# A chunked recurrence: score products alternate between row halves of TensorE, the old state is scaled on GpSimd, low-rank factors share the array, dense steps stand between chain steps

## The chip, the cores and the metric

One Trainium2 chip, one of its cores. The metric is the device time of one execution in microseconds (us); lower is better. TensorE (PE in the rows; PEld is its weight load) does the matrix products, VectorE (DVE), ScalarE (ACT) and GpSimd (POOL) the rest, SyncE (SP) issues nearly all transfers.

## What is computed

Two transformer layers and a third block on 512 tokens of width 1024, all in float32. The part that the change touches is the time mixing of the first layer:

```python
r, k, v = xr @ w_rkv[0], xk @ w_rkv[1], xv @ w_rkv[2]
w = -softplus(-(w0 + tanh(xw @ w1) @ w2)) - 0.5        # w1: 1024 x 64
a = sigmoid(a0 + (xa @ a1) @ a2)                       # a1: 1024 x 64
...
def step(S, inp):                                      # 16 heads, S is 64 x 64 per head
    sa = einsum('bhij,bhj->bhi', S, -kk_t)
    S = S * w_t + sa * b_t + v_t * k_t
    return S, einsum('bhij,bhj->bhi', S, r_t)
```

followed by a group norm, a gate and an output projection. Before and after it stand gated feed-forward networks, and behind it window attention and the third block, which the change does not touch.

## The kernel before

The recurrence runs over chunks of 64 tokens. A unit is 128 tokens (two chunks, c = 0 and 1) and 8 of the 16 heads; there are 8 units, n = 0 to 7, two for each 128 tokens, and m = 2 (n // 2) + c numbers the chunks from 0 to 7. For a unit four stages are written as generators that yield between steps:

- stage a: cumulative decays (`psc`), then the scores (`sc`, L1072). A pair of heads lies on 128 partitions, one on the lower 64 rows and one on the upper; f = 0 to 3 numbers the pairs. For each chunk the products of the four lower heads go to one bank of PSUM, a yield follows, then the four upper ones go to another. DVE multiplies each bank by a mask (L1074). The pool `pa` has two banks. Then come transposes (`pt`).
- stage b: inverts the triangular blocks, first on DVE, one 16-block per lane, then by small products in 32 x 32 tiles (`psG`, `psW`).
- stage c: per chunk a chain: products with the old state and the scores (`xy`, L1181 and L1184), L1189, L1194, then the new state in `st`: for each row half a product of the identity with the old state (L1203) and four products (L1206) are summed in PSUM, and DVE multiplies by the decay (L1209). The chunk behind it reads the new state.
- stage d: group norm and gate; the unit's output goes to DRAM (L1247).

`Rwkv.run` calls them in rounds. `chain(n)` strings the four stages together; stage x of unit n starts behind stage x of unit n - 1; at most three units (later two) hold a slot. In a round every live chain makes one step, then three dense steps follow (four in the second part). The dense side of the first part is `dense(1, ...)`: projections and low-rank paths of the second 256 tokens, beside units 0 to 3. The dense side of the second part is `first_half(...)`: output projection, norm and feed-forward network of the first 256 tokens, beside units 4 to 7; it reads the outputs of units 0 to 3. `dense(0, ...)` has run before the recurrence, without a chain beside it. What comes behind the second part (the output projection of the second 256 tokens) reads the outputs of units 4 to 7.

In `dense`, `mixes` makes the mixed inputs xr, xw, xa, xk, xv, xg in this order, 8 tiles each, on DVE. `low_rank` sums 8 products with xw and 8 with xa in one bank; the weight block for xw is w1 beside 64 columns of zeros, the one for xa is 64 columns of zeros beside a1, so that the results lie on the lower and on the upper partitions. A float32 product is two instructions on PE in the rows (the 128 score products stand as x256).

The order in which each engine runs its instructions is made by the framework, from the order in which they are emitted and a simulated timeline (`schedule_with_timeline_sim=True`, L2021): an instruction can overtake those emitted before it on its engine.

Of the kernel before, what the change touches and what calls it, by code (L numbers as in the profile page):

```python
# [17 lines left out]
P = 128  # L18
T = 512
# [53 lines left out]


class Turns:
    """tiles of PSUM from these pools in turn"""
# [9 lines left out]
class Net:  # L86
    def __init__(self, tc, ctx, ins, outs):
# [21 lines left out]
        # 1 / rms of h by tokens, for products with h before its norm's division  # L109
# [36 lines left out]
    def weights(self, src, pool=None, cols=1024, hl=None):  # L146
        """src: DRAM AP [P, cols] -> (hi, lo) tiles [P, cols] of float32r"""
# [29 lines left out]
    def rstd(self, ps, dim, out=None):  # L177
        """1 / sqrt(sum / dim + eps) of the sums, on every partition; in ps itself or in out"""
# [37 lines left out]
    def sumsq(self, pieces, n):  # L216
        """sum over pieces of piece^2, [P, n]"""
# [28 lines left out]
    def rms(self, half, onpe=False):  # L246
        """self.rx of this half"""
# [12 lines left out]
    def pairs(self, pool, tag="xn", **k):  # L260
        """8 tiles [P, 2, 256] out of four slots"""
# [29 lines left out]
    def post(self, g, half):  # L291
        """emit g now for the first half, later for the second, beside the phase that follows"""
# [20 lines left out]
    def ffn(self, idx, gpost, after_half, side=(), early=()):  # L313
        nc = self.nc
        win, wout = self.ins["ffn_w_in"][idx], self.ins["ffn_w_out"][idx]
        with ExitStack() as es:
# [4 lines left out]
            for fh in range(2):  # L321
# [12 lines left out]
                # the first tiles by halves of the tokens, beside the tail of the phase before  # L334
# [40 lines left out]
                # out: 88 blocks (d, f) in 11 pieces of 8  # L375
# [35 lines left out]
class Halves:  # L411
    """an FFN by halves of the tokens: its steps as generators"""
# [4 lines left out]
    def hidden(self, f, halves, w=None):  # L417
        """hidden tile f for each (x, a, half): x 8 times [P, 2, 256], a the pair of hi and lo [P, 256]"""
# [17 lines left out]
    def out(self, fh, halves):  # L436
        """output tiles of half fh of the hidden ones; halves: (a by f, sink(d, psum))"""
# [15 lines left out]
def lay(inputs):  # L453
    """host-side layout only"""
# [11 lines left out]
    # query heads in the order in which tile t = 4 a + j holds heads (2 a, j) and (2 a + 1, j)  # L466
# [11 lines left out]
    # second block: columns of the input projection by tiles; the rotary key part four times over  # L478
# [21 lines left out]
    l1 = np.stack([np.concatenate([g("rwkv_w1")[0], z64], 1), np.concatenate([z64, g("rwkv_a1")[0]], 1), g("rwkv_g1")[0]])  # L500
    o["lora1"] = np.ascontiguousarray(l1.reshape(3, 8, 128, 128).transpose(0, 2, 1, 3)).reshape(3, 128, 1024)
# [11 lines left out]
class Rwkv:  # L513
    def __init__(self, N):
# [3 lines left out]
        # 64-blocks of ones on the diagonal, and the inclusive triangle within chunks of 64  # L518
# [4 lines left out]
        # tri[s, t] = 1 where t >= s within the same chunk  # L523
# [3 lines left out]
        # masks of the scores, rows s (both halves alike), columns [r | a] for even chunks and [a | r] for odd ones  # L527
# [16 lines left out]
    def unorm(self, gcol, half):  # L544
# [8 lines left out]
        if half == 0:  # L553
            # on demand of the projections
# [18 lines left out]
    def dense(self, hf, tmp, exact, mx, mxe):  # L573
        """r, k, v and the low-rank paths of one half of the tokens, to DRAM; emitted in steps.
        exact: projections with products of the float32 operands as they are, the others with those of their
        halves hi and lo. mx, mxe: how many mixed inputs of each kind fit, and how to make room for one"""
# [21 lines left out]
        def mixes():  # L598
            for i, out, ex in order:
                for k in range(KT):  # L600
# [20 lines left out]
        # the weights in the order of their use, loaded ahead of it  # L621
        srcs = [(N.ins["w_rkvo"][j, o], j in exact) for j in range(3) for o in range(KT)] + [(N.ins["lora1"][2], True), (N.ins["lora2"][1], True)]
# [13 lines left out]
        def proj(j, x, post):  # L636
            """post(o, psum) is a generator that runs beside the next products"""
            ex = j in exact
            o = 0
            while o < KT:  # L640
                # the first two together: their inputs come one by one
# [31 lines left out]
        def low_rank():  # L673
            psl = mmt()
            ws = [weights(N.ins["lora1"][j], True) for j in range(2)]
            yield from lora(ws[0], xw, psl[:, :n], True, False)
            yield from lora(ws[1], xa, psl[:, :n], False, True)
# [27 lines left out]
        def post_k(o, ps):  # L705
# [5 lines left out]
            # k (a k_a + 1 - k_a)  # L711
# [11 lines left out]
            # kk over its norm, and times a  # L723
# [43 lines left out]
        order = [(0, xr, 0 in exact), (1, xw, True), (4, xa, True), (2, xk, 1 in exact), (3, xv, 2 in exact), (5, xg, True)]  # L767
# [32 lines left out]
    def run(self, h_spill, gpost, gpre, ffn, gffn, after_half):  # L800
        """the block, and the FFN that follows it"""
# [44 lines left out]
        def step():  # L846
            live[:] = [g for g in live if next(g, live) is not live]
# [7 lines left out]
        more = True  # L855
        run(islice(side, 1))
        while more or ("d", 2) not in at:
# [3 lines left out]
            step()  # L861
            for _ in range(3):
                more = more and next(side, side) is not side
# [9 lines left out]
        more = True  # L873
        while n < 8 or live:
# [3 lines left out]
            step()  # L878
            if ("d", 3) in at:
                for _ in range(4):  # L880
                    more = more and next(side, side) is not side
        for _ in side if more else ():
            pass
# [60 lines left out]
    def out_half(self, hf, y, m, h_spill, gpost, after):  # L944
        """output projection, norm and residual of one half of the tokens"""
# [14 lines left out]
    def first_half(self, h_spill, gpost, gpre, ff, m, a, xA):  # L960
        """for the first half of the tokens: output projection, and the lower half of the hidden tiles"""
# [23 lines left out]
class Core:  # L985
    """recurrence over chunks of 64 tokens; unit n: tokens 128 (n // 2) on, heads 8 (n % 2) on"""

    def __init__(self, R, dram, cx):
# [16 lines left out]
        # 64-blocks of 16 (chunk, head) pairs, 4160 apart: their diagonal 16-blocks are then 1040 apart throughout  # L1005
        self.us, self.wsd = ([dram.tile([16, 4160], F32, name=f"{x}{n}") for n in range(2)] * 4 for x in ("us", "wsd"))
        zero = self.S0[0].rearrange("p a b -> p (a b)")[:, 0:520]
        for w in self.wsd[:2]:
            nc.gpsimd.dma_start(out=w.rearrange("a (b e) -> (a b) e", e=520), in_=zero)
# [12 lines left out]
    def load(self, nm, n, t, c=None):  # L1022
        """feature-major [P, 4, tokens of chunk c or of both]"""
# [4 lines left out]
    def stage_a(self, n, G):  # L1028
# [9 lines left out]
        # columns of chunk c: [r | a] and [k | b] for the even one, [a | r] and [b | k] for the odd one  # L1038
# [23 lines left out]
        # scores  # L1062
# [3 lines left out]
        for c in range(2):  # L1066
            s = st_.tile([P, 8, P], F32, tag=f"S{c}", name="S")
            for p in range(2):
                ps = pa("sc").rearrange("p (f t) -> p f t", t=P)
                rows = slice(64 * p, 64 * p + 64)  # L1070
                for f in range(4):
                    nc.tensor.matmul(ps[:, f, :], lhsT=two(kb, rows, f, c), rhs=two(ar, rows, f, c), start=f == 0, stop=True, skip_group_check=True)  # L1072
                yield
                nc.vector.tensor_tensor(out=s[:, p:8:2, :], in0=ps, in1=R.mask[c][:, None, :].to_broadcast([P, 4, P]), op=ALU.mult)  # L1074
# [950 lines left out]
```

## Time and profile before

| | us |
|---|---|
| median of 3 runs | 2792.01 |
| lowest and highest | 2785.80, 2796.27 |
| span of the profiled execution | 2792.8 |

The profiled execution's span is 0.8 us above the median of the three runs. In the trace the rows of a timeline join neighbouring instructions of one line: the time is from the start of the first to the end of the last. PE's products are pipelined and their ends are modelled, so that what one costs is read from start to start. PEclk is the granted clock as a share of 2.4 GHz.

### The profile page before, as it was taken

The page shows a single profiled execution, that of the slowest core. Times are in us where ns is not written, and L with a number is a line of the kernel's source. Part 1 is how long each engine was busy: PE and PEld are TensorE (multiplying, and loading weights), DVE is VectorE, ACT ScalarE, POOL GpSimd, SP SyncE. Part 2 cuts the span into 40 slices and gives each one's busy share as a digit, 9 for nine tenths or more (in the row PEclk, how much of TensorE's full clock was granted, in tenths as well). Part 3 has the DMA queues.
Part 4 walks back from the last instruction along what each step waited for, and adds up shares of the span by engine and source line. Part 5 has one row for each costly group of instructions (what it writes and reads, how often), then busy time and mean ns, then how long its engine had stood idle before and what let it go on. Part 6 is the DMA issues. An engine that isn't in the chain of part 4 may idle for free.

```text
span 2792.8 us, 43747 instructions
## 1 busy us (share of the span) xinstructions
PE 2709.0 (97%) x17518; PEld 2355.8 (84%) x17518; DVE 1472.3 (53%) x2964; ACT 1169.9 (42%) x2073; POOL 12.5 (0%) x30
## 2 busy tenths in 40 slices
PE   8999998899999999999999999999999999999998
PEld 7888887778888999999988889789888898777887
DVE  7724466455547546448652446547524465334555
ACT  5223326244346554335532234446322334454643
POOL 0000000000000000000000000000000000000000
PEclk9999999998999999999999999899999999999999
DMA  6622316854574453235442233002322232123333
GB/s 211 211 96 97 113 65 215 251 164 117 176 228 129 133 190 136 91 107 181 133 144 91 98 106 136 34 18 89 107 98 95 101 104 101 64 69 103 116 124 101
DMA packets 207716, 345.26 MB, mean 124 GB/s; under 512 B 66196, under 2 KB 136212, under 8 KB 207512
## 3 DMA queue, kind: packets, MB, share of 16 engines
q1 hardware_dynamic: 206920, 341.65, 37.6%
q8 instruction: 138, 2.26, 0.3%
q14 instruction: 66, 0.54, 0.1%
q0 software_dynamic: 160, 0.53, 0.0%
q10 hardware_dynamic: 432, 0.28, 0.0%
HBM read 299.56 MB, written 41.26 MB: 122 GB/s over the span
## 4 chain that ended last, share of the span: by engine, by line
PE 88%; DMA 4%; DVE 4%; ACT 3%; issue 1%; SPq 0%; DVEq 0%; ACTq 0%
PE gu L165 11%; PE gu L164 11%; PE gu L166 11%; PE o L164 8%; PE o L166 8%; PE o L165 8%; PE ps L594 4%; PE ps L166 2%; PE ps L164 2%; PE ps L165 2%; PE psg L164 1%; PE psg L165 1%; PE psg L166 1%; PE po L1417 1%; PE sc L1072 1%
## 5 line engine op out<-in xcount | busy, mean ns | idle before, releaser
L153 ACT ACTIVATE whl<-wr 128x1024 fp32r<-128x1024 f32 x417 | 439.0, 1059 | 729.9 <-PE gu L166 408.1
L154 DVE TENSOR_TENSOR whl<-wr,whl 128x1024 fp32r<-128x1024 f32 x417 | 507.9, 1222 | 373.3 <-ACT whl L153 370.9
L164 PE MATMUL gu<-xn,whl 128*128 128x512 f32 (+1 forms) x1200 | 436.5, 366 | 7.8 <-ACT xn L242 7.1
L165 PE MATMUL gu<-xn,whl 128*128 128x512 f32 (+1 forms) x1200 | 439.8, 367 | 3.6 <-DVE xn L243 3.6
L166 PE MATMUL gu<-xn,whl 128*128 128x512 f32 (+1 forms) x1200 | 438.6, 366 | 0.8 <-DVE whl L154 0.8
L166 PE MATMUL o<-a,whl 128*128 128x256 f32 (+1 forms) x906 | 297.9, 330 | 0.0
L165 PE MATMUL o<-a,whl 128*128 128x256 f32 (+1 forms) x906 | 297.2, 329 | 0.0
L164 PE MATMUL o<-a,whl 128*128 128x256 f32 (+1 forms) x906 | 296.4, 329 | 0.0
L164 PEld LDWEIGHTS gu<-xn,whl 128*128 128x128 f32 x1200 | 226.8, 190 | 43.8 <-ACT xn L242 7.3
L165 PEld LDWEIGHTS gu<-xn,whl 128*128 128x128 f32 x1200 | 228.3, 190 | 40.2 <-DVE xn L243 4.8
L166 PEld LDWEIGHTS gu<-xn,whl 128*128 128x128 f32 x1200 | 228.4, 190 | 37.1 <-DVE whl L154 1.2
L165 PE MATMUL gu<-pair,whl 128*128 128x256 f32 x704 | 200.1, 285 | 1.1 <-DVE pair L243 1.1
L166 PE MATMUL gu<-pair,whl 128*128 128x256 f32 x704 | 198.3, 282 | 1.2 <-DVE whl L154 1.2
L164 PE MATMUL gu<-pair,whl 128*128 128x256 f32 x704 | 199.4, 285 | 0.0
L165 PEld LDWEIGHTS o<-a,whl 128*128 128x128 f32 x906 | 170.8, 189 | 17.1
L166 PEld LDWEIGHTS o<-a,whl 128*128 128x128 f32 x906 | 170.8, 189 | 16.9
L164 PEld LDWEIGHTS o<-a,whl 128*128 128x128 f32 x906 | 170.4, 189 | 17.1
L594 PE MATMUL ps<-mxe,wraw 128*128 128x256 f32 x608 | 153.9, 405 | 11.5 <-DVE mxe L608 5.8
L594 PEld LDWEIGHTS ps<-mxe,wraw 128*128 128x128 f32 x608 | 119.4, 203 | 33.1 <-DVE mxe L608 6.0
L166 PEld LDWEIGHTS gu<-pair,whl 128*128 128x128 f32 x704 | 133.4, 189 | 2.1 <-DVE whl L154 1.4
L165 PEld LDWEIGHTS gu<-pair,whl 128*128 128x128 f32 x704 | 133.1, 189 | 2.3 <-DVE pair L243 1.7
L164 PEld LDWEIGHTS gu<-pair,whl 128*128 128x128 f32 x704 | 132.6, 189 | 1.5 <-issue 0.4
(438 smaller groups left out, 4783.5 us busy)
## 6 DMA issues: line engine op xcount, KB each, us to landing
wr<-in_ffn_w_in_dram SPq DMA_DIRECT2D x204, 512.0 KB, 3.5
wr<-in_ffn_w_out_dram SPq DMA_DIRECT2D x99, 512.0 KB, 3.5
wr<-in_w_in_dram SPq DMA_DIRECT2D x38, 512.0 KB, 3.5
wraw<-in_w_rkvo_dram SPq DMA_DIRECT2D x32, 512.0 KB, 4.3
wr<-in_w_rkvo_dram SPq DMA_DIRECT2D x32, 512.0 KB, 4.4
wr<-in_w_ada_dram SPq DMA_DIRECT2D x24, 512.0 KB, 4.3
wr<-in_w_qo_dram SPq DMA_DIRECT2D x16, 512.0 KB, 3.5
gates<-xf SPq DMA_DIRECT2D x48, 128.0 KB, 1.8
```

The costliest lines, as they stand in the source:

```text
L153: nc.scalar.activation(out=hl[:, 0, :cols], in_=raw[:, :cols], func=AF.Copy)
L154: nc.vector.tensor_tensor(out=hl[:, 1, :cols], in0=raw[:, :cols], in1=hl[:, 0, :cols].bitcast(F32), op=ALU.subtract)
L164: nc.tensor.matmul(ps, lhsT=wh, rhs=xh, start=start, stop=False, **k)
L165: nc.tensor.matmul(ps, lhsT=wh, rhs=xl, start=False, stop=False, **k)
L166: nc.tensor.matmul(ps, lhsT=wl, rhs=xh, start=False, stop=stop, **k)
L594: nc.tensor.matmul(ps, lhsT=w[:, b * P:(b + 1) * P], rhs=x, start=start, stop=stop)
L1072: nc.tensor.matmul(ps[:, f, :], lhsT=two(kb, rows, f, c), rhs=two(ar, rows, f, c), start=f == 0, stop=True, skip_group_check=True)
L1417: nc.tensor.matmul(po[:, n, r, :], lhsT=pT[:, r, sb * W:(sb + 1) * W], rhs=v[:, n - 1 + sb, d0:d0 + 64], start=n == 0 and r == 0, stop=sb ...
```

## The change

Four edits in the recurrence, and two small ones that go with them:

- scores: both banks of a chunk are taken at once, and the eight products alternate between the lower and the upper rows; one yield instead of two per chunk;
- state: for m = 1 to 6 GpSimd scales the old state by the decay in two instructions at the start of the chunk, the identity products are gone, DVE scales the sum from PSUM in one instruction and adds the scaled old state in two;
- low rank: one weight block holds w1 beside a1; for each k two products of 64 columns each go to the two column halves of the array; the mixed inputs xw and xa are made in turn; a step takes both;
- rounds: behind each live chain's step one dense step, up to the round's number, the rest at the end;
- the zeros for `wsd` are written from SP's queue instead of GpSimd's, and the scratch for software-made transfers is cut to 2048 bytes.

All other lines of the diff take comments away.

```diff
-    l1 = np.stack([np.concatenate([g("rwkv_w1")[0], z64], 1), np.concatenate([z64, g("rwkv_a1")[0]], 1), g("rwkv_g1")[0]])
+    l1 = np.stack([np.concatenate([g("rwkv_w1")[0], g("rwkv_a1")[0]], 1), g("rwkv_g1")[0]])
...
-            for i, out, ex in order:
-                for k in range(KT):
+            for i, out, ex in ((i, out, ex) for group in order for _ in range(KT) for i, out, ex in group):
+                k = len(out)
...
-            ws = [weights(N.ins["lora1"][j], True) for j in range(2)]
-            yield from lora(ws[0], xw, psl[:, :n], True, False)
-            yield from lora(ws[1], xa, psl[:, :n], False, True)
+            w = weights(N.ins["lora1"][0], True)
+            for k in range(KT):
+                for j, x in enumerate((xw, xa)):
+                    need(x, k)
+                    q = slice(64 * j, 64 * j + 64)
+                    nc.tensor.matmul(psl[q, :n], lhsT=w[:, k * P:(k + 1) * P][:, q], rhs=x[k], start=k == 0, stop=k == KT - 1, skip_group_check=True, tile_position=(0, 64 * j))
+                    live[1] -= 1
...
+                feed()
+                feed()
+                yield
...
-        def step():
-            live[:] = [g for g in live if next(g, live) is not live]
+        def step(steps, dense):
+            for g in list(live):
+                if next(g, live) is live:
+                    live.remove(g)
+                for _ in range(min(steps, 1)):
+                    dense()
+                    steps -= 1
+            for _ in range(steps):
+                dense()
...
-            nc.gpsimd.dma_start(out=w.rearrange("a (b e) -> (a b) e", e=520), in_=zero)
+            nc.sync.dma_start(out=w.rearrange("a (b e) -> (a b) e", e=520), in_=zero)
...
+            pss = [pa("sc").rearrange("p (f t) -> p f t", t=P) for _ in range(2)]
+            for f in range(4):
+                for p in range(2):
+                    rows = slice(64 * p, 64 * p + 64)
+                    nc.tensor.matmul(pss[p][:, f, :], lhsT=two(kb, rows, f, c), rhs=two(ar, rows, f, c), start=f == 0, stop=True, skip_group_check=True)
+            yield
             for p in range(2):
-                ps = pa("sc").rearrange("p (f t) -> p f t", t=P)
-                rows = slice(64 * p, 64 * p + 64)
-                for f in range(4):
-                    nc.tensor.matmul(ps[:, f, :], lhsT=two(kb, rows, f, c), rhs=two(ar, rows, f, c), start=f == 0, stop=True, skip_group_check=True)
-                yield
-                nc.vector.tensor_tensor(out=s[:, p:8:2, :], in0=ps, in1=R.mask[c][:, None, :].to_broadcast([P, 4, P]), op=ALU.mult)
+                nc.vector.tensor_tensor(out=s[:, p:8:2, :], in0=pss[p], in1=R.mask[c][:, None, :].to_broadcast([P, 4, P]), op=ALU.mult)
...
+            if 0 < m < 7:
+                sp = tp.tile([P, 4, C], F32, tag="sp", name="sp", bufs=2)
+                for hh in range(2):
+                    q = slice(64 * hh, 64 * hh + 64)
+                    nc.gpsimd.tensor_tensor(out=sp[q], in0=s0[q, :, q], in1=pcol[q, :, c, :].to_broadcast([64, 4, C]), op=ALU.mult)
...
-                    if m:
-                        nc.tensor.matmul(st[q], lhsT=N.ident[q, q], rhs=s0[q, :, q], start=True, stop=False, skip_group_check=True, tile_position=(64 * hh, 64 * hh))
...
+                if m:
+                    sn = tp.tile([P, 4, C], F32, tag="sn", name="sn")
+                    nc.vector.tensor_tensor(out=sn, in0=st, in1=pcol[:, :, c, :].to_broadcast([P, 4, C]), op=ALU.mult)
                 for hh in range(2):
                     q = slice(64 * hh, 64 * hh + 64)
-                    nc.vector.tensor_tensor(out=s0n[q, :, q], in0=st[q], in1=pcol[q, :, c, :].to_broadcast([64, 4, C]), op=ALU.mult)
+                    if m:
+                        nc.vector.tensor_tensor(out=s0n[q, :, q], in0=sn[q], in1=sp[q], op=ALU.add)
+                    else:
+                        nc.vector.tensor_tensor(out=s0n[q, :, q], in0=st[q], in1=pcol[q, :, c, :].to_broadcast([64, 4, C]), op=ALU.mult)
```

## Rows read from the trace of the kernel before

**Rows 1.** The page, part 1: busy time, share of the span, instructions of TensorE.
```profile
PE 2709.0 (97%) x17518; PEld 2355.8 (84%) x17518; DVE 1472.3 (53%) x2964; ACT 1169.9 (42%) x2073; POOL 12.5 (0%) x30
```

**Rows 2.** Stretches of the recurrence, all engines; columns as in the first line.
```profile
core 0: us, PE busy (x) PEld busy (x) DVE busy (x) ACT busy (x) POOL busy (x), PEclk, DMA share, GB/s
545.00:794.00 249.00, 243.69 (x2365) 200.10 (x2364) 135.16 (x415) 103.97 (x239) 3.11 (x6) 0.94 0.58 164
794.00:808.00 14.00, 11.01 (x146) 9.72 (x143) 1.83 (x5) 4.66 (x12) 0.52 (x1) 0.62 0.79 266
...
838.00:860.00 22.00, 22.00 (x256) 19.36 (x254) 14.64 (x36) 14.29 (x32) 0.52 (x1) 0.84 0.34 99
860.00:1018.00 158.00, 155.85 (x1621) 144.08 (x1621) 95.16 (x197) 85.31 (x161) 1.04 (x2) 0.99 0.45 143
```

**Rows 3.** Seven stretches at a lower TensorE clock: the longest but one, the sum.
```profile
650.60:660.80 10.20, 10.20 (x77) 8.19 (x73) 3.34 (x6) 3.89 (x11) 0.00 (x0) 0.50 0.41 113
...
sum 47.60, PE 47.15 PEld 39.15 DVE 17.68 ACT 20.70 POOL 0.52; mean PE 6.74 PEld 5.59 DVE 2.53 ACT 2.96 POOL 0.07
```

**Rows 4.** Timeline of PE around score products: start, us, engine, line, tiles, count.
```profile
548.93 1.71 PE L1072 MATMUL sc<-ar,kb 64*128 64x128 f32 x16
...
602.05 1.16 PE L1072 MATMUL sc<-ar,kb 64*128 64x128 f32 x8
603.13 1.13 PE L594 MATMUL ps<-lo,wraw 128*128 128x256 f32 x4
604.19 1.16 PE L1072 MATMUL sc<-ar,kb 64*128 64x128 f32 x8
```

**Rows 5.** Stretches again, for the score products of L1072 alone.
```profile
838.00:860.00 22.00, 4.02 (x32) 3.45 (x32) 0.84 0.34 99
...
sum 473.00, PE 33.41 PEld 27.96; mean PE 6.68 PEld 5.59
```

**Rows 6.** Timeline of PE around one old-state product of L1203.
```profile
734.02 0.63 PE L1206 MATMUL st<-vsa,kt 128*64 128x64 f32 x8
734.59 0.64 PE L1203 MATMUL st<-S,ident 64*64 64x256 f32 x2
735.16 0.68 PE L1206 MATMUL st<-vsa,kt 128*64 128x64 f32 x8
```

**Rows 7.** The old-state products: min/median/max ns, first and last start.
```profile
L1203 PE MATMUL st<-S,ident x48: 375/402/687, 623.3 to 978.8; 64*64 64x256 f32 x48
```

**Rows 8.** Timeline of PE: runs of float32 products of the dense side.
```profile
403.80 6.85 PE L594 MATMUL ps<-mxe,wraw 128*128 128x256 f32 x31
...
519.03 3.62 PE L594 MATMUL ps<-mxe,wraw 128*128 128x256 f32 x16
...
718.09 3.72 PE L594 MATMUL ps<-mxe,wraw 128*128 128x256 f32 x16
```

**Rows 9.** Timeline of PE where two column halves of the array are in use.
```profile
750.51 0.27 PE L1206 MATMUL st<-vsa,kt 128*64 128x64 f32 x1
750.56 0.22 PE L1194 MATMUL xy<-vsa,S 128*64 128x64 f32 x1
750.62 0.22 PE L1206 MATMUL st<-vsa,kt 128*64 128x64 f32 x1
```

**Rows 10.** The state update on DVE; on POOL, the nearest operation by size.
```profile
L1209 DVE TENSOR_TENSOR S<-st,pcol x28: 406/422/429, 617.4 to 980.2; 64x256 f32<-64x256 f32 x28
...
L1003 POOL TENSOR_SCALAR_AFFINE_SELECT eye<-ones 64x256 f32<-64x256 f32 x1 | 0.5, 498 | 0.0
```

**Rows 11.** Timeline of POOL at the start of the recurrence.
```profile
530.68 1.25 POOL L1009 DMA_DIRECT2D wsd<-S  x2 [13.77 <-DVE S L1001]
```

**Rows 12.** Timelines of SP and PE: outputs of units stored, first product behind them.
```profile
767.51 1.22 SPq L1247 DMA_DIRECT2D y<-yo  x2
...
1010.32 0.38 SPq L1247 DMA_DIRECT2D y<-yo  x1
...
1017.96 0.39 PE L164 MATMUL o<-pair,whl 128*128 128x256 f32 x1 [1.42 <-ACT whl L153]
```

More of the change, by code (lines that the diff above doesn't have):

```diff
@@ L499, in lay @@
     z64 = np.zeros((1024, 64), np.float32)
-    l1 = np.stack([np.concatenate([g("rwkv_w1")[0], z64], 1), np.concatenate([z64, g("rwkv_a1")[0]], 1), g("rwkv_g1")[0]])
-    o["lora1"] = np.ascontiguousarray(l1.reshape(3, 8, 128, 128).transpose(0, 2, 1, 3)).reshape(3, 128, 1024)
+    l1 = np.stack([np.concatenate([g("rwkv_w1")[0], g("rwkv_a1")[0]], 1), g("rwkv_g1")[0]])
+    o["lora1"] = np.ascontiguousarray(l1.reshape(2, 8, 128, 128).transpose(0, 2, 1, 3)).reshape(2, 128, 1024)
     o["lora2"] = np.stack([np.concatenate([z64.T, g("rwkv_a2")[0]], 0), g("rwkv_g2")[0]])
@@ L598, in mixes @@
         def mixes():
-            for i, out, ex in order:
-                for k in range(KT):
+            for i, out, ex in ((i, out, ex) for group in order for _ in range(KT) for i, out, ex in group):
+                k = len(out)
+                if True:
                     if hf == 0:
@@ L619, in need @@
                 next(ahead)
-        srcs = [(N.ins["w_rkvo"][j, o], j in exact) for j in range(3) for o in range(KT)] + [(N.ins["lora1"][2], True), (N.ins["lora2"][1], True)]
+        srcs = [(N.ins["w_rkvo"][j, o], j in exact) for j in range(3) for o in range(KT)] + [(N.ins["lora1"][1], True), (N.ins["lora2"][1], True)]
         loaded, posts = [], []
@@ L674, in low_rank @@
             psl = mmt()
-            ws = [weights(N.ins["lora1"][j], True) for j in range(2)]
-            yield from lora(ws[0], xw, psl[:, :n], True, False)
-            yield from lora(ws[1], xa, psl[:, :n], False, True)
+            w = weights(N.ins["lora1"][0], True)
[5 more added lines that the diff above has]
+                    live[1] -= 1
+                if k % 3 == 2:
+                    after()
+                feed()
+                feed()
+                yield
             nc.scalar.activation(out=lw[0:64], in_=psl[0:64, :n], func=AF.Tanh)
@@ L766, in dense @@
         xr, xw, xa, xk, xv, xg = [], [], [], [], [], []
-        order = [(0, xr, 0 in exact), (1, xw, True), (4, xa, True), (2, xk, 1 in exact), (3, xv, 2 in exact), (5, xg, True)]
+        order = [[(0, xr, 0 in exact)], [(1, xw, True), (4, xa, True)], [(2, xk, 1 in exact)], [(3, xv, 2 in exact)], [(5, xg, True)]]
         ahead = mixes()
@@ L854, in run, with dense @@
         side = self.dense(1, tmp, (0, 1, 2), None, (16, lambda: mxe.tile([P, 256], F32, tag="mxe", name="mxe")))
-        more = True
+        more = [True]
+        def dense():
+            more[0] = more[0] and next(side, side) is not side
         run(islice(side, 1))
-        while more or ("d", 2) not in at:
+        while more[0] or ("d", 2) not in at:
             if n < 4 and free and (n == 0 or ("a", n - 1) in at):
@@ L860, in run @@
                 n += 1
-            step()
-            for _ in range(3):
-                more = more and next(side, side) is not side
+            step(3, dense)
         third.close()
@@ L872, in run @@
         side = self.first_half(h_spill, gpost, gpre, ff, m, a, xA)
-        more = True
+        more = [True]
         while n < 8 or live:
@@ L877, in run @@
                 n += 1
[L878 to L882, printed above, removed]
+            step(4 if ("d", 3) in at else 0, dense)
+        for _ in side if more[0] else ():
             pass
@@ L1201, in stage_c @@
                     q = slice(64 * hh, 64 * hh + 64)
-                    if m:
-                        nc.tensor.matmul(st[q], lhsT=N.ident[q, q], rhs=s0[q, :, q], start=True, stop=False, skip_group_check=True, tile_position=(64 * hh, 64 * hh))
                     for f in range(4):
                         h = 2 * f + hh
-                        nc.tensor.matmul(st[q, f, :], lhsT=kt[:, c, f, q], rhs=vsa[c][:, h * C:(h + 1) * C], start=m == 0 and f == 0, stop=True, skip_group_check=True, tile_position=(0, 64 * hh))
+                        nc.tensor.matmul(st[q, f, :], lhsT=kt[:, c, f, q], rhs=vsa[c][:, h * C:(h + 1) * C], start=f == 0, stop=True, skip_group_check=True, tile_position=(0, 64 * hh))
+                if m:
+                    sn = tp.tile([P, 4, C], F32, tag="sn", name="sn")
+                    nc.vector.tensor_tensor(out=sn, in0=st, in1=pcol[:, :, c, :].to_broadcast([P, 4, C]), op=ALU.mult)
                 for hh in range(2):
                     q = slice(64 * hh, 64 * hh + 64)
-                    nc.vector.tensor_tensor(out=s0n[q, :, q], in0=st[q], in1=pcol[q, :, c, :].to_broadcast([64, 4, C]), op=ALU.mult)
+                    if m:
+                        nc.vector.tensor_tensor(out=s0n[q, :, q], in0=sn[q], in1=sp[q], op=ALU.add)
+                    else:
+                        nc.vector.tensor_tensor(out=s0n[q, :, q], in0=st[q], in1=pcol[q, :, c, :].to_broadcast([64, 4, C]), op=ALU.mult)
                 yield
@@ L2012 @@
     from concourse.bass_utils import run_bass_kernel_spmd
-    nc = bacc.Bacc("TRN2", target_bir_lowering=False, num_devices=1)
+    nc = bacc.Bacc("TRN2", target_bir_lowering=False, num_devices=1, dynamic_dma_scratch_size=2048)
     arrays, ins = {}, {}
```

## The prediction, made before the changed kernel had run

> **What bounds the kernel now.** The page's first part shows TensorE busy for 97% of the span and no other engine above 53% [rows 1]; ends of products are modelled, so I looked at stretches next. In the first part of the recurrence, 545 to 794 us, PE is busy for 244 of 249 us, DVE for 135, ACT for 104, POOL for 3; in the second, 860 to 1018, PE for 156 of 158 [rows 2]. So PE's work sets the pace, and a product that goes is worth its spacing, if what follows on PE is ready. Two stretches differ. From 794 to 808 the dense side of the first part is used up and the weights of the second are not there yet: PE does chain steps alone, at a granted clock of 0.62. From 838 to 860 the first half's norm runs, and PE fills the time with chain steps [rows 2]. PE work that goes from these 36 us is worth little. The third view is the clock: in seven stretches of the recurrence, together 47.6 us, 1.2 GHz were granted (PEclk 0.50), most with PE nominally busy but with small products [rows 3].
>
> Then the chain's slack. Unit 3's output is stored at 767.5, 26 us before the dense side ends: in the first part the chain does not set the end. Unit 7's is stored at 1010.3 and the first product that needs the next weights starts at 1018.0 [rows 12]; with the stored output's way back into SBUF between, chain and dense side end there nearly together. So time saved in the second part counts only if the chain gets shorter too.
>
> **Scores.** A block of eight instructions (one row half of a chunk) takes 1.16 us on its own, twice with other work between [rows 4]. The line is busy for 33.4 us in all, 4.0 of it between 838 and 860 [rows 5]. After the change 16 blocks (8 units, 2 chunks) of sixteen remain. If the two halves run fully side by side, a block takes 1.16 us as eight do now; where two blocks happened to meet, sixteen took 1.71 us [rows 4], which bounds it from the other side. So 18.6 to 27.4 us are left, and 14.8 to 6.0 are saved. I take 1.2 us a block, 14 saved, because alternation offers a partner to every instruction, while the met blocks overlapped only at their seam. Less half of the 4.0 between 838 and 860: 12. Chunk 1's products now need both banks of `pa`, so they wait for two mask products on DVE; the three dense steps of a round (each 0.43 us, two instructions at 0.215, see below) cover 1.3 us. If that cover is gone I price the wait at one block each, 8 x 1.2 = 10 us.
>
> **Old state.** L1203 has 48 instructions, 24 pairs [rows 7]. One pair, from its start to that of the next block, takes 735.16 - 734.59 = 0.57 us: 13.7 us. In the row the four heads' products (L1206) stand on both sides; the block behind it takes 0.68 instead of 0.63 us, as entering another tile shape costs about 0.05, and leaving costs about 0.1 [rows 6]. Where both neighbours are alike (about half of the pairs) 0.15 x 12 = 1.8 us go too. So 13.7 to 15.5, less two pairs in the slack stretches: 13.5. DVE does three instructions of about 0.42 us instead of two [rows 10], 12 x 0.42 = 5 us more in all on an engine that is half idle; per chunk it lengthens the chain by 0.4. The POOL product has no row; one input of 64x256 took 0.50 us there [rows 10], two inputs I bound by 0.5 and 1.0, two instructions per chunk by 1 and 2 us. It is ready as soon as the old state is and wanted after four dependent steps, so it costs nothing; uncovered it costs 12 x 2 = 24 us on the chain. Queued behind it on POOL is only the next unit's clearing of `vsa`. By the Trainium skill, page "GPSIMD Engine Reference", section 3.1, a two-input product takes about 2.6 cycles per element at 1.2 GHz there, an estimate of 0.55 us for 256 elements; the sum would not change, and no run here has shown it yet.
>
> **Low rank.** The spacing of dense products is (6.85 - 3.62) / 15 = 0.215 us [rows 8]. Now 16 products a half, two instructions each, two halves: 64 x 0.215 = 13.8 us. After: 16 steps of two products on column halves. Side by side a step takes 2 x 0.215 = 0.43, one after the other 0.86. That column halves overlap is seen where L1206 and L1194 start in turn, 0.05 us apart, each 0.22 long [rows 9]. But every step lies between full-array projections: a run of sixteen of these takes 3.72 us behind a block of other shape and 3.62 behind one of the same [rows 8], so 0.1 for coming back; and before another shape the last spacing is 604.19 - (603.13 + 1.13 - 0.38) = 0.31 instead of 0.215 [rows 4], so 0.1 for leaving (0.38 is 3.62 less 15 spacings). With 0.05 for entering and 0.1 for leaving the pair, a lone step costs 0.43 + 0.35 = 0.78: 16 x 0.78 = 12.5, a gain of 1.3. One after the other: 16 x 1.21 = 19.4, a loss of 5.6. Gathered without switches: 6.9 left, a gain of 6.9. I take a gain of 1. One weight transfer less per half hides in the loading ahead: nothing.
>
> **Dense steps between.** The change puts a dense step between chains of the same round. Counting yields, about 50 rounds have two or more chains at work; each may get one more switch, 0.1 to leave and 0.1 to come back: 0 to 10 us. As dense and chain blocks take turns already [rows 4], I take 3. Against that, fewer chain-only stretches may spare low clock: at half rate the 34 us of rows 3 outside 797 to 811 cost up to 17 us. I take 2.
>
> **The zeros.** Two writes, 1.25 us on POOL behind a wait of 13.8 us for DVE's clearing [rows 11], now stand in SP's queue among weight loads. If SP waits there, loads behind it are late by that: 0 to 2 us; I take 1, as PE waits at that point anyway.
>
> **Sum.** 12 + 13.5 + 1 - 3 + 2 - 1 = 24.5. PE's neighbours must be ready to fill the freed time; of 249 us in the first part 5 are waits now, and with a tenth of PE's work gone I give back 2.5. That leaves 22: from the profiled span of 2792.8 (0.8 above the median) to 2770.
>
> **The rivals.**
> 1. The freed time does not survive. In the second part about 8 us of the sum arise (8 pairs and 4 chunks of scores), and chain and dense side end together there; with 6 more lost to waits the time is 2784. For it: the 7.7 us between unit 7's store and the next product [rows 12]. Against it: stage a has 6 steps instead of 8, so that the second part's chain ends after 52 rounds instead of 57, 20 dense steps sooner.
> 2. The low clock goes as well, the low-rank steps are gathered: 12 of the 17 us and 6 more, 2752. For it: the dips stand in chain-only work [rows 3]. Against it: less PE work also means more waiting.
> 3. Slower: the chain falls behind. Dense steps now stand ahead of a second chain's step; if the order on PE serves them first, they are used up early, and the rest of the chain runs alone, as from 794 to 808, which holds one chunk: 14 us [rows 2]. Two units behind are four chunks, 56 us, and 8 for the last output's way; the dense side would end at 1018 - 22 - 4 x 5 (their PE work, half of 11 busy us at half clock each) = 976, the part at 1040, the kernel at 2814. It decides from three chunks behind on. Against it: the chain's 26 us of slack in the first part.
> 4. Strict order. The overlap at the seam, 0.55 us for eight more instructions [rows 4], shows a later half starting before the earlier one has issued its last. If it did not, each score block took one spacing more (16 x 0.11) and each low-rank step one more (16 x 0.215): 5 us, 2775. The Trainium skill, page "TensorE: Matmul & The Clock Gate", Part 3, has products start strictly in program order, which is this case; the rows speak against it.
>
> That the change does not do what it says is part of the bounds: the framework may pull the eight products apart, as it has split some blocks now.
>
> **How the numbers follow.** 2770 gets 0.55, its own range 2760 to 2782; rival 1 0.23, rival 2 0.10, rival 3 0.07, rival 4 0.05. Range: 2746 to 2798, leaving out most of rival 3 and the far end of rival 2. About 0.5%, 14 us, is what a measurement of this kernel can tell from no change: faster means below 2778, slower above 2806. Faster: 0.48 + 0.10 + 0.04 + 0.04 of rival 1 = 0.66. Same: 0.07 + 0.19 + 0.01 = 0.27. Slower: 0.07.
>
> **What would show it.** Right: L1072's successor busy for some 19 us in 16 blocks; no 64*64 64x256 products; the first part about 16 us shorter, the second about 6; the stretches behind 1018 unchanged in length. Low-rank steps as pairs, 0.78 us each. Wrong: score blocks of 1.7 us; more PE idle time before L1189 or the state; unit 7 stored well behind the last dense product; more low clock; a POOL product above 2 us.

## The result and the profile after

The changed kernel took 2768.4 us (median of 5, 2756.3 to 2773.1) against 2792.0 before: a ratio of 0.9905, 95% interval 0.9887 to 0.9922. The forecast was 2770. The profiled execution of after spans 2766.7 us.

First the page, part 1, the row of [rows 1]; then two stretches of each kernel, from 380 us to the first product that needs the next weights (before first), for all engines:

```profile
PE 2680.9 (97%) x17470; PEld 2330.6 (84%) x17470; DVE 1477.9 (53%) x2976; ACT 1167.9 (42%) x2072; POOL 27.4 (1%) x52
```

```profile
core 0: us, PE busy (x) PEld busy (x) DVE busy (x) ACT busy (x) POOL busy (x), PEclk, DMA share, GB/s
380.00:1018.00 638.00, 600.60 (x5475) 526.02 (x5473) 362.40 (x928) 294.79 (x617) 10.03 (x19) 0.94 0.56 170
1018.00:2792.00 1774.00, 1738.60 (x10153) 1512.78 (x10153) 907.50 (x1680) 747.13 (x1265) 1.66 (x5) 0.98 0.31 104
```

```profile
380.00:988.40 608.40, 569.18 (x5411) 500.57 (x5409) 366.09 (x935) 292.30 (x613) 24.97 (x41) 0.94 0.60 177
988.40:2766.00 1777.60, 1741.74 (x10153) 1513.13 (x10153) 907.43 (x1680) 746.76 (x1265) 1.62 (x5) 0.98 0.32 104
```

PE lost 31.4 us of work around the recurrence and the path got 29.6 us shorter; what PE does not fill went from 37.4 (638.00 - 600.60) to 39.2 us. 3.6 us came back behind it, in unchanged code.

Where it went, by five stretches: the first part with its dense side, the stretch until the output projection has weights, that projection, the norm, the second part. Before, then after:

```profile
534.20:793.80 259.60, 253.69 (x2395) 208.32 (x2396) 137.43 (x420) 105.47 (x244) 4.15 (x8) 0.93 0.60 173
793.80:807.70 13.90, 10.91 (x147) 9.65 (x146) 1.57 (x4) 4.56 (x11) 0.52 (x1) 0.63 0.77 260
807.70:838.60 30.90, 30.90 (x268) 28.96 (x266) 16.41 (x20) 16.31 (x29) 0.00 (x0) 0.95 0.75 237
838.60:860.10 21.50, 21.50 (x252) 18.86 (x250) 14.10 (x37) 14.39 (x32) 0.52 (x1) 0.84 0.34 99
860.10:1018.00 157.90, 155.75 (x1621) 143.98 (x1620) 95.11 (x197) 85.20 (x160) 1.04 (x2) 0.99 0.45 143
```

```profile
531.90:783.30 251.40, 244.28 (x2457) 201.69 (x2458) 139.15 (x425) 107.99 (x248) 12.12 (x20) 0.92 0.64 179
783.30:789.90 6.60, 6.23 (x144) 5.66 (x144) 2.51 (x4) 2.98 (x7) 3.20 (x5) 1.00 0.95 298
789.90:824.90 35.00, 34.97 (x373) 33.03 (x369) 21.34 (x33) 23.42 (x45) 0.52 (x1) 1.00 0.77 239
824.90:838.70 13.80, 11.13 (x125) 9.61 (x123) 9.99 (x25) 10.10 (x23) 3.54 (x5) 1.00 0.83 235
838.70:988.40 149.70, 145.50 (x1537) 137.59 (x1536) 95.60 (x199) 79.22 (x149) 1.99 (x3) 0.98 0.47 146
```

The two parts gained 8.2 us each, the three stretches between them 10.9; the other 2.3 stand before the first part, where the low-rank products of the first 256 tokens are. In the norm's stretch PE was busy all the time before and has 2.7 us of waits now.

Two things in these rows change how they are to be read. The first is the clock. Before, the three stretches between the parts lost 13.9 x 0.37 + 30.9 x 0.05 + 21.5 x 0.16 = 10.1 us to it, after nothing: at full clock they took 56.2 us and take 55.4. So nearly all of their 10.9 us is clock. At full clock each of the two parts gained about 10. The changed kernel's second profiled execution shows the three stretches at 1.00 again:

```profile
783.70:838.90 55.20, 52.39 (x635) 48.35 (x634) 33.92 (x60) 36.49 (x74) 7.26 (x11) 1.00 0.79 242
```

The second is that chain steps moved. The first part holds 62 instructions of PE more than before, though the change takes some away; the projection's stretch holds 105 more, the norm's 127 and the second part 84 fewer.

From the first part's end to the output projection one weight load leaves SP earlier. SP's queue, before, then after:

```profile
796.46 1.78 SPq L791 DMA_DIRECT2D g<-ev  x4
798.29 1.40 SPq L152 DMA_DIRECT2D wr<-in_w_rkvo_dram  x3
```

```profile
782.91 0.45 SPq L152 DMA_DIRECT2D wr<-in_w_rkvo_dram  x1
783.79 1.36 SPq L801 DMA_DIRECT2D g<-ev  x2
785.24 0.93 SPq L152 DMA_DIRECT2D wr<-in_w_rkvo_dram  x2
```

Before, all stores of the gate stood ahead of the first weight load; after, one load stands ahead of the last two. This order is the framework's.

### The profile page after: what moved, and what is told of

It reads as the page before. It is cut to its first block, busy times and chain, and to the rows that moved or that the text cites. A ratio compares the mean times of both kernels' runs of the same rounds, so it can differ in the third digit from the quotient of the medians.

```text
span 2766.7 us, 43687 instructions
## 1 busy us (share of the span) xinstructions
PE 2680.9 (97%) x17470; PEld 2330.6 (84%) x17470; DVE 1477.9 (53%) x2976; ACT 1167.9 (42%) x2072; POOL 27.4 (1%) x52
## 4 chain that ended last, share of the span: by engine, by line
PE 88%; DVE 4%; DMA 3%; ACT 3%; issue 1%; SPq 0%; DVEq 0%; ACTq 0%
PE gu L165 11%; PE gu L164 11%; PE gu L166 11%; PE o L164 8%; PE o L166 8%; PE o L165 8%; PE ps L594 4%; PE ps L166 2%; PE ps L165 2%; PE ps L164 2%; PE psg L164 2%; PE psg L165 1%; PE psg L166 1%; PE po L1443 1%; PE z L1756 1%
## 5 line engine op out<-in xcount | busy, mean ns | idle before, releaser
L594 PE MATMUL ps<-mxe,wraw 128*128 128x256 f32 x544 | 144.4, 416 | 15.2 <-DVE mxe L609 7.5
L594 PEld LDWEIGHTS ps<-mxe,wraw 128*128 128x128 f32 x544 | 108.9, 208 | 38.1 <-DVE mxe L609 7.7
```

The source lines that it names most:

```text
L594: nc.tensor.matmul(ps, lhsT=w[:, b * P:(b + 1) * P], rhs=x, start=start, stop=stop)
```

## The experiments

In the table every execution's span is split by its mean granted clock c: "full clock" is span x c, "lost" is span x (1 - c), as if PE set the pace throughout. Both are means over 5 to 12 executions (17 to 26 of before), with standard errors of 0.5 to 1.7 and 1.1 to 2.7 us.

| kernel | median us | ratio, 95% interval | full clock | lost |
|---|---|---|---|---|
| before, beside the first four | 2793.4 | | 2722.0 | 70.6 |
| before + scores | 2779.0 | 0.9951 [0.9934, 0.9969] | 2715.0 | 62.5 |
| before + state + small edits | 2789.9 | 0.9987 [0.9974, 1.0001] | 2714.5 | 73.2 |
| before + small edits | 2800.9 | 1.0023 [1.0007, 1.0039] | 2723.7 | 76.3 |
| before + low rank | 2782.1 | 0.9960 [0.9947, 0.9973] | 2715.7 | 64.9 |
| before, beside the next four | 2793.5 | | 2720.7 | 70.4 |
| before + rounds | 2795.5 | 1.0002 [0.9985, 1.0018] | 2721.3 | 71.5 |
| after - rounds | 2770.2 | 0.9916 [0.9892, 0.9939] | 2698.4 | 70.1 |
| after, halves in turn | 2782.0 | 0.9967 [0.9949, 0.9986] | 2701.4 | 80.0 |
| after, state on DVE | 2773.8 | 0.9929 [0.9903, 0.9954] | 2697.6 | 74.9 |
| before, beside the last four | 2795.3 | | 2722.1 | 71.8 |
| after again | 2768.9 | 0.9903 [0.9888, 0.9918] | 2703.6 | 62.0 |
| after - scores | 2773.0 | 0.9924 [0.9904, 0.9943] | 2708.9 | 62.4 |
| after, pairs in turn | 2776.2 | 0.9934 [0.9916, 0.9952] | 2707.7 | 66.6 |
| before + zeros on SP | 2789.3 | 0.9981 [0.9968, 0.9995] | 2719.1 | 68.8 |

**The edits one at a time.** Scores:

```diff
+            for f in range(4):
+                for p in range(2):
...
+            yield
```

> The kernel before with the scores' edit alone. Theory (PE work that goes counts at its spacing): a full block of sixteen products takes 1.1 to 1.2 us from its start to the next block's, the line some 20 us in place of 33; 10 to 14 us are saved, a ratio of 0.995 to 0.996, and the stretch without dense work behind the first part (13.9 us before) stays within 3 us. Rival (the 23.6 us came mainly from stretches that got shorter around the recurrence, by another order on the queues): 0 to 5 us.

14.4 us less, just above the 10 to 14 of the theory, but only 7.0 us are at full clock; 8.1 are clock (the two are means and need not add up to the difference of medians). The stretch behind the first part shrank too, from 13.9 to 7.7 us.

State, with the small edits:

```diff
+                    nc.gpsimd.tensor_tensor(out=sp[q], in0=s0[q, :, q], in1=pcol[q, :, c, :].to_broadcast([64, 4, C]), op=ALU.mult)
-                        nc.tensor.matmul(st[q], lhsT=N.ident[q, q], rhs=s0[q, :, q], start=True, stop=False, skip_group_check=True, tile_position=(64 * hh, 64 * hh))
```

> The kernel before with the state's edit, and with the two small ones (zeros on SP, scratch of 2048 bytes), since the scaled states take room in SBUF that only the smaller scratch gives. Theory: 24 pairs at 0.57 us go, 11 to 15 us below the kernel with the small edits alone, a ratio to before of 0.995 to 0.996; the POOL product takes 0.5 to 1.0 us. Rival (DVE's third instruction lengthens the chain by as much as PE gains): 0 to 4 us.

3.5 us less than before, 11.0 less than the kernel with the small edits alone, 9.2 of it at full clock. Against that base the theory's gain is there; its ratio to before is not.

The small edits alone:

```diff
-            nc.gpsimd.dma_start(out=w.rearrange("a (b e) -> (a b) e", e=520), in_=zero)
+            nc.sync.dma_start(out=w.rearrange("a (b e) -> (a b) e", e=520), in_=zero)
...
-    nc = bacc.Bacc("TRN2", target_bir_lowering=False, num_devices=1)
+    nc = bacc.Bacc("TRN2", target_bir_lowering=False, num_devices=1, dynamic_dma_scratch_size=2048)
```

> The kernel before with the two small edits alone: zeros on SP, scratch of 2048 bytes. Theory: nothing, within 3 us. Rival 1: other addresses in SBUF let the first weight loads of the output projection leave SP's queue earlier, so that the stretch without dense work shrinks from 13.9 to about 7 us, as it did with the whole change: 7 us less, ratio 0.9975. Rival 2: the zeros hold up the weight loads behind them on SP: 1 to 2 us more.

7.5 us more. None of the three said so: the stretch behind the first part did shrink, to 5.6 us, but the first part took 280.1 instead of 259.6, at a granted clock of 0.90 and with 2510 instead of 2395 instructions of PE in it (in the profiled execution, which at 2809.6 us is one of the longest). The zeros alone:

```diff
-            nc.gpsimd.dma_start(out=w.rearrange("a (b e) -> (a b) e", e=520), in_=zero)
+            nc.sync.dma_start(out=w.rearrange("a (b e) -> (a b) e", e=520), in_=zero)
```

> The kernel before with the zeros written from SP's queue alone; the scratch stays. With both small edits the time was 2801 us, 7 above before. Theory (the zeros hold up SP's queue by 1 to 2 us, as predicted): 2793 to 2797. Rival 1 (that wait is the whole 7 us): 2798 to 2804. Rival 2 (it is the smaller scratch with its other addresses and the order that follows from them): 2790 to 2794.

2789.3, just below rival 2's window and 6.0 below the kernel before beside it: the zeros cost nothing by themselves, so the 7.5 us came with the scratch, or with the two edits together. PE's work is the same in these two and in before, but in both its order differs from before's at many places. So with the same work, orders alone made 2789 to 2801 us, 4.6 us apart at full clock and 7.5 in what the clock lost. A single edit's gain below that can't be told from the new order it brings.

Low rank:

```diff
-            yield from lora(ws[0], xw, psl[:, :n], True, False)
-            yield from lora(ws[1], xa, psl[:, :n], False, True)
+            for k in range(KT):
+                for j, x in enumerate((xw, xa)):
```

> The kernel before with the low-rank edit alone. The whole change showed 9.2 us for the 64 products, in pairs of 0.58 us or gathered, where 13.8 were spent before. Theory: 4 to 5 us less, ratio 0.998. The prediction had 1 us less (16 lone steps of 0.78). Rival: the new order of the mixed inputs (xw and xa in turn) delays projections, and nothing or 2 us more comes out.

11.3 us less, 6.3 at full clock. The theory, made from after's rows, is near the full-clock part; 5.7 us are clock, which it did not have.

Rounds, alone and taken out of the changed kernel:

```diff
-            step()
-            for _ in range(3):
-                more = more and next(side, side) is not side
+            step(3, dense)
```

> The kernel before with the edit of the rounds alone: dense steps between the chains' steps. Theory as predicted: added switches cost 3 (0 to 10) us, spared low clock gives 2 back, so -2 to +8 us. Rival: this order is what shortened the stretch behind the first part (13.9 to 6.6 us) and the norm's stretch (21.5 to 13.8 us) with the whole change: 7 to 15 us less, ratio 0.995 to 0.9975.

> The changed kernel with the rounds as before: all chains make a step, then the dense steps follow. Theory: within 5 us of the changed kernel (2764 to 2772, ratio to before 0.990 to 0.993), with slightly fewer tile-shape switches. Rival (the dense steps between keep PE filled and the clock up): the stretch behind the first part is about 14 us again, low clock in the recurrence rises from 72 back to over 80 us, and the time is 2776 to 2786.

Nothing in either case that can be measured in the time. Taken out of the changed kernel, the full-clock time is 5.2 us lower and the clock loses 8.1 more, which would be the switches and the spared clock of the prediction; added to the kernel before, neither shows (0.6 more at full clock, 1.1 more lost). With standard errors of 2 and 3 us on the first pair, the two prices are not shown.

**Alternation or adjacency.**

```diff
-            for f in range(4):
-                for p in range(2):
+            for p in range(2):
+                for f in range(4):
```

> The changed kernel, but with a chunk's eight score products in the old order: the four lower heads, then the four upper ones, still in one step with both banks. Theory (an instruction overtakes only its neighbour, so alternation is needed): the halves overlap at their seam only, a block of sixteen takes 1.7 us in place of 1.16, 16 x 0.55 = 9 us more than the changed kernel, ratio to before 0.993 to 0.994. Rival (it is enough that both halves stand together on PE's queue): blocks of 1.16 us and the changed kernel's time.

```diff
-            for f in range(4):
-                for p in range(2):
+            for f, p in ((f, p) for f0 in (0, 2) for p in range(2) for f in (f0, f0 + 1)):
```

> The changed kernel with the eight score products in turns of two: two lower heads, two upper ones, two lower, two upper; four instructions of a half stand together in place of two. With eight instructions together the halves saved 0.53 us at their one seam (2.17 for two blocks apart, 1.64 together), about five spacings of 0.108. Theory (a half's instructions start up to some five places ahead of their turn): four in a row still overlap fully, blocks of 1.1 to 1.2 us, and the changed kernel's time within 4 us. Rival (only the neighbouring product is overtaken): 1.3 to 1.6 us a block, 3 to 8 us more.

Timelines of PE, a full block and what follows it: after, pairs in turn, halves in turn.

```profile
586.78 1.16 PE L1088 MATMUL sc<-ar,kb 64*128 64x128 f32 x16
587.87 1.99 PE L594 MATMUL ps<-mxe,wraw 128*128 128x256 f32 x8
```

```profile
625.46 1.26 PE L1088 MATMUL sc<-ar,kb 64*128 64x128 f32 x16
626.65 0.70 PE L594 MATMUL ps<-mxe,wraw 128*128 128x256 f32 x2
```

```profile
625.79 1.71 PE L1088 MATMUL sc<-ar,kb 64*128 64x128 f32 x16
627.43 0.50 PE L1216 MATMUL xy<-vsa,S 128*64 128x64 f32 x5
```

From start to the next start: 1.09, 1.19, 1.64 us. Eight alone took 1.08 [rows 4], so alternating halves are entirely side by side. In the third block the second half's first instruction starts at 626.345, when three of the first half's eight (626.451, 626.563, 626.674) are still to start: that is the seam. Both theories had their block price right. The times went up by 13 and 7 us, more than the theories had; but for halves in turn none of it is at full clock (2701.4 against 2703.6), and the framework leaves only some blocks whole. In the time of the kernel the block price can't be separated there from another order and another clock. In the line's busy time it shows. For L1088 alone, pairs in turn, halves in turn, and then the changed kernel with the scores as before (the next run); the columns are PE busy, PEld busy, PEclk, DMA share, GB/s:

```profile
530.00:1000.00 470.00, 29.04 (x256) 23.76 (x256) 0.95 0.58 174
530.00:1000.00 470.00, 32.73 (x256) 27.15 (x256) 0.92 0.57 169
530.00:1000.00 470.00, 35.62 (x256) 30.08 (x256) 0.94 0.58 172
```

The changed kernel has 26.05 us (shown below): 3.0, 6.7 and 9.6 us less. Some low clock is in all four.

**Taking the scores out of the changed kernel.**

```diff
+                ps = pa("sc").rearrange("p (f t) -> p f t", t=P)
...
+                yield
```

> The changed kernel with the scores as before: eight products of one row half, a yield, eight of the other. Theory: the scores' part comes back whole, 10 to 14 us above the changed kernel, ratio to before 0.994 to 0.996, and at least as slow as the version with both halves in one step but in turn (2782). Rival (the edits share their gains): 5 us or less above the changed kernel.

4.2 us more, 5.3 at full clock: the rival's number, though the intervals of the two ratios overlap, and that the edits share their gains is not shown. At full clock the scores' edit is worth 7.0 us added to before and 5.3 within the whole, with standard errors of 1 and 2 us. The rest of the difference between 14 and 4 us is clock: 8.1 us there, 0.4 here.

**The old state on DVE.**

```diff
-                    nc.gpsimd.tensor_tensor(out=sp[q], in0=s0[q, :, q], in1=pcol[q, :, c, :].to_broadcast([64, 4, C]), op=ALU.mult)
+                    nc.vector.tensor_tensor(out=sp[q], in0=s0[q, :, q], in1=pcol[q, :, c, :].to_broadcast([64, 4, C]), op=ALU.mult)
```

> The changed kernel with the old state scaled on DVE in place of POOL: two more instructions of some 0.25 to 0.45 us per chunk, 24 in all, early in the chunk. Theory (DVE is half idle and they are wanted four dependent steps later): within 4 us of the changed kernel. Rival (DVE's queue holds up the chain's mask and state instructions): 24 x 0.4 = 10 us more.

5 us more with intervals that overlap, and 6.0 less at full clock: no cost of a wait shows. The intervals exclude neither the theory's 4 us nor the rival's 10, but in both traces no instruction is listed as having waited for this product. The instruction on POOL, then DVE's two kinds, in after (min/median/max ns, first and last start):

```profile
L1198 POOL TENSOR_TENSOR sp<-S,pcol x24: 608/614/949, 614.5 to 848.3; 64x256 f32<-64x256 f32 x24
```

```profile
L1229 DVE TENSOR_TENSOR sn<-st,pcol x12: 401/425/425, 629.2 to 944.1; 128x256 f32<-128x256 f32 x12
```

```profile
L1233 DVE TENSOR_TENSOR S<-sn,sp x24: 406/420/425, 630.8 to 945.1; 64x256 f32<-64x256 f32 x24
```

**The changed kernel again.**

> The changed kernel once more, beside the three others and with the clock of every execution. Theory: about 2768 us, ratio to before 0.989 to 0.992. What it is to tell apart, as time at full clock (span times mean granted clock) and time lost to the clock (the rest): in the theory the whole gain is PE work and stands in the first number, some 18 to 24 us below before's 2721, with the second near before's 70 us. Rival: a third or more of the gain is clock, the second number near 60 us.

26.5 us less by medians. By means 28.3: 18.5 at full clock, 9.9 clock, a third. The rival holds, just. But clock losses of 62 to 80 us were seen in kernels with nearly the same work, so this third can't be credited to the edits rather than to the order that they brought.

Added one at a time, the edits come to the whole: 14.4 (scores) + 11.0 (state, against the small edits) + 11.3 (low rank) - 2.0 (rounds) - 7.5 (small edits) = 27.2 us by medians, and 20.2 at full clock against 18.5. Each of the single gains is uncertain by 3 to 6 us.

## Why the forecast held, step by step

**Scores (12 us counted).** The price of a block was right: 1.2 taken, 1.09 measured. The count was not. The framework pulled the products apart into 22 blocks, where 16 were counted, and the first two units meet in one block of 32 that waits for DVE's mask products. Its second half, and the stretch of low clock that it stands in:

```profile
565.03 3.09 PE L1088 MATMUL sc<-ar,kb 64*128 64x128 f32 x16 [1.43 <-DVE S L1091]
```

```profile
564.40:574.60 10.20, 9.57 (x29) 7.34 (x30) 6.24 (x24) 2.38 (x3) 0.00 (x0) 0.50 0.51 149
```

So the cover by dense steps that the prediction named was gone there; it cost 1.4 us once, and half of the 3.09 us is the clock of 0.50. The line's busy time fell by 7.4 us, from 33.41 [rows 5] to the number below, where 19 was forecast. With the clock of other stretches mixed in, 7.4 is a rough measure; against the changed kernel with the scores as before it is 9.6.

```profile
531.90:988.40 456.50, 26.05 (x256) 21.50 (x256) 0.95 0.61 176
```

**Old state (13.5 counted).** L1203's 48 instructions are gone and the blocks beside them got cheaper. Busy times of before's L1206 and of after's L1226, each from the first part's start to the next weights:

```profile
534.20:1018.00 483.80, 20.21 (x224) 16.30 (x224) 0.94 0.56 166
```

```profile
531.90:988.40 456.50, 14.61 (x224) 12.34 (x224) 0.95 0.61 176
```

From start to next start both lines together went from 30.3 to 14.7 us, at the upper end of the 13.7 to 15.5. Alone, 9.2 us of it was seen in the kernel's time at full clock; where the rest went is not shown. POOL's product took 0.61 us, inside 0.5 to 1.0. The Trainium skill, page "GPSIMD Engine Reference", section 3.1, gives about 2.6 cycles per element; the 0.55 us estimated from it are 0.06 short of this. DVE's three instructions took 0.42 us each, as taken.

**Low rank (1 counted).** The mis-sized term. One product alone (x2), then a step of both (x4), each between dense ones (timeline of PE, after):

```profile
419.88 0.65 PE L681 MATMUL ps<-mxe,wraw 128*64 128x256 f32 x2
420.46 0.70 PE L594 MATMUL ps<-mxe,wraw 128*128 128x256 f32 x2
421.09 0.65 PE L681 MATMUL ps<-mxe,wraw 128*64 128x256 f32 x4
421.67 1.13 PE L594 MATMUL ps<-mxe,wraw 128*128 128x256 f32 x4
```

Four instructions take 0.58 us, two take the same: the halves are side by side. The two dense instructions between take 0.63 us from start to start, 0.20 more than two spacings of 0.215, for coming back and leaving. So a lone step costs 0.58 + 0.20 = 0.78, as forecast. What was wrong is the count: the 32 products stand in 10 blocks, of 2 to 16 instructions, and not in 16 lone steps. The 64 instructions took 9.2 us and the dense ones beside them 1.6 more (0.105 nine times behind a block, 0.094 seven times ahead of one), 10.8 in place of 13.8, between "gathered" (6.9) and "lone" (12.5). The gain is 3 by these rows, not 1; the 6.3 us that the edit alone brought at full clock are more than that, and the rest is not explained.

**Dense between (-3, +2).** Together nothing that can be measured, as against -1 in the sum. The run without the edit has both signs (5.2 at full clock, 8.1 spared), the run with the edit alone has neither.

**Zeros (-1).** No cost. In the changed kernel SP issued them at 394.6 us, with no wait in the row, long before the loads that were meant; in the run with the zeros alone they stood at 532.0 us among those loads, and that kernel was no slower. After, then zeros alone:

```profile
L1025 SPq DMA_DIRECT2D wsd<-S x2: 351/385/419, 394.6 to 395.0; - x2
```

```profile
L1009 SPq DMA_DIRECT2D wsd<-S x2: 423/468/513, 532.0 to 532.6; - x2
```

**Filling (-2.5).** 1.8 us more of waits (37.4 to 39.2): about right.

**Where.** Here the prediction failed: the first part got 8.2 us shorter, not 16, the second 8.2, not 6, and the slack stretches, said to be worth little, 10.9. It took the chain's work as staying in its stretch, and it took 2 us for the clock. In the rows chain steps moved forward, out of the second part and the norm's stretch, which fits a first part that gained less and a second that gained more; at full clock the two gained about 20 us together. The slack stretches gave 10.1 of their 10.9 us by the clock, 0.63, 0.95 and 0.84 before and 1.00 after. That PE work which goes from them is worth little is not contradicted: at full clock they got 0.8 us shorter. The low clock there stood in [rows 2]; two of the seven stretches of rows 3, in before, hold it:

```profile
797.40:811.00 13.60, 13.15 (x131) 11.63 (x132) 3.91 (x5) 5.75 (x12) 0.52 (x1) 0.50 0.94 297
852.00:858.80 6.80, 6.80 (x43) 6.13 (x44) 5.08 (x15) 5.55 (x12) 0.00 (x0) 0.50 0.49 106
```

In the profiled executions other stretches lost more to the clock after than before, so that this is not the gain of the whole kernel.

**The rivals.** 1 (the freed time does not survive): it did, with 8.2 us in the second part. 3 (the chain falls behind): the last store of unit 7's output leaves at 975.5 us, 12.8 us before the next weights' first product, where there were 7.6 [rows 12]:

```profile
L1273 SPq DMA_DIRECT2D y<-yo x16: 359/364/528, 641.5 to 975.5; - x16
```

```profile
988.36 0.39 PE L164 MATMUL o<-pair,whl 128*128 128x256 f32 x1 [1.42 <-ACT whl L153]
```

4 (strict order) is refuted by the blocks of 1.09 us, where it gives 1.19, and by the seam at 626.345. The Trainium skill, page "TensorE: Matmul & The Clock Gate", Part 3, has products start in strict order; between row halves the measurement decides against it. 2 is the half-right one: the low rank was gathered in part, and the clock lost some 10 us less. In the profiled pair 6.8 of those 10.1 us lay at 797 to 811, which the prediction had set aside, and the rest at 852 to 859. So the total came out right in part by luck, as a sum of errors: at full clock the terms gave 20 (12 + 13.5 + 1 - 3 - 1 - 2.5) and 18.5 was measured, scores (7.0 alone) and state (9.2) short, low rank (6.3) over; the clock gave 9.9 where 2 was taken.

**Left open.** Why an order loses 62 or 80 us to the clock. Dips stood in chain-only work with PE nominally busy in before [rows 3], but after has a chain-only stretch at 1.00 (783.3 to 789.9 us).

## What to carry to other kernels

Price an edit by start-to-start spacings, and count with the order that the framework will really make, not with the one emitted: blocks were pulled apart and met. Before a stretch's gain is credited to work that went, take its clock out of it and count its instructions: here work had moved and the clock had risen. A price for changing tile shape has to count the products on both sides of the block. Where a new order alone moves the time by 0.4%, split times into full clock and lost before an edit is credited with them, and test an edit both added to the old kernel and taken out of the new one.

## What the runs showed of the hardware

- Products on the two row halves run entirely side by side when they alternate (1.09 us for sixteen, 1.08 for eight); four of one half in a row cost one spacing more (1.19); eight in a row overlap only at the seam (1.64). An instruction started while three of the other half, emitted ahead of it, were still to start.
- Column halves did the same: 0.58 us for one 64-column product of two instructions and for two such products. Between two such blocks two dense instructions took 0.63 us instead of 0.43.
- With the same PE work, another order of instructions changed the time lost to the granted clock from 68.8 to 76.3 us (zeros on SP alone, and with the smaller scratch), and over all kernels here it ranged from 62 to 80.
